# Down projections: loads of residual rows and of the third product's operands held behind the operand unit in use

## The chip, the core and the metric

The kernel runs on one core of a Trainium2 chip. A core has five engines that run their own instruction queues: TensorE (PE in the profile; its weight loads are PEld), VectorE (DVE), ScalarE (ACT), GpSimd (POOL) and SyncE (SP), which here issues nearly all transfers between DRAM and the on-chip memory. The engines wait for each other through semaphores; an instruction that waits holds up everything behind it in the same queue. The metric is the device time of one execution in microseconds; lower is better. It is given as the median of several runs, and one more execution is recorded by the hardware profiler.

## The reference

The program is a decoder trunk of two layers over 1024 tokens with 1024 features. The first layer mixes tokens with a gated linear recurrence, the second with sliding-window attention; both end with a gated feed-forward network, and every sub-layer is followed by a layer norm of a scaled residual. What matters here is the end of each layer:

```python
def conv_ffn(h, w_in, conv_w, conv_b, w_out):
    u = h @ w_in                                   # 1024 -> 2 * 2816
    u = <causal depthwise convolution of width 3>(u) + conv_b
    a, b = jnp.split(u, 2, axis=-1)
    return (jax.nn.silu(a) * b) @ w_out            # 2816 -> 1024

    # in reference(), for each layer:
    h = layer_norm(ALPHA * h + mix, ln_mix_g[layer], ln_mix_b[layer])
    ff = conv_ffn(h, ffn_w_in[layer], ffn_conv_w[layer], ffn_conv_b[layer], ffn_w_out[layer])
    h = layer_norm(ALPHA * h + ff, ln_ffn_g[layer], ln_ffn_b[layer])
```

All arrays are float32. The change is in how the last product, the down projection with `w_out`, is fed.

## The kernel before

**Split operands.** Each float32 operand is split into an upper half of reduced precision (`split`, L216, a cast on ScalarE) and the rest (`low_part`, L164, a subtract on VectorE). A product is then three matmuls (`mm3`, L189 to L191: upper by upper, upper by lower, lower by upper), into one bank of the accumulator memory.

**The up projection** (`Up`) computes 22 blocks of 128 features for both halves of the gate, applies the convolution (L483 on ScalarE, L485 on VectorE) in tiles `Y[:, 0..6]`, multiplies the halves (L490) and writes each block to DRAM as `gd` (L491). The tile `Y[:, 7]` serves as a buffer for weights. Before it, the normalised mixer output, which is the residual of this sub-layer, was written to DRAM as `ynd`, eight rows of tiles of 512 KB each, because Y was needed for the convolution.

**The down projection** (`Down`) multiplies the 1024 x 2816 gate output with `w_out` by a scheme of seven half-size products in place of eight, in the order `ORDER = [1, 2, 5, 6, 7, 3, 4]`; here they are called the first to the seventh. Each sums over 11 operand units (H = 11). A unit (`operands`, L554) is a 128 x 512 block of the gate output and one of the weights, 256 KB each, or sums of such blocks. It is loaded by SP into one of four raw buffers (three `rx` and one `rd`, in turn), cast to its upper half by ScalarE (L216) and its rest is made by VectorE (L164). The result goes to one of 15 operand slots, in `HL`, `HT` and `T`. The third product adds two blocks (L569) in a tile `R`, which holds a pair of 128 x 512 blocks for each of the 11 units: `R[:, 0, k]` is loaded from `gd` (L544), `R[:, 1, k]` from sums of weights that were made earlier and stand in DRAM as `bsd` (L552).

**The steps.** A step is one `mm3`: one unit k with one of four token blocks tb, that is four banks to a product and 44 steps to a product, about 0.68 us each. The steps go through the units in order, four steps each, for the first six units (`late` is 6 in the first product); then tb by tb through units 6 to 10. So units 6 to 10 are met in five steps in a row, 24 to 28. The banks of a product are emptied into Y (`evacuate`, L605 to L609), those of products 1 and 2 through a list `later`.

**The residual.** Before anything is added to it, Y must hold the residual rows: each is loaded from `ynd` (L652), multiplied by the gain row and shifted by the bias row of the layer norm before (L653, two instructions on VectorE a row, called shifts here). These two rows of parameters are loaded (L295) into parts of R: `free_rows(3)` and `free_rows(4)` are `R[:, 0, 6..7]` and `R[:, 0, 8..9]`. The shifts stand first in the list `later`; `run` takes one from the list after steps 11, 15, 19 and so on, in the order of rows 0, 4, 1, 5, 2, 6, 3, 7. A row's load is called together with its first shift.

**What sets the order.** Only TensorE's queue is in the order in which the code is written:

```python
    with tile.TileContext(nc) as tc, tc.manual_schedule(engines={mybir.EngineType.PE}):
```

In the down projections the queues of the other engines are laid out when the kernel is built: a planner runs through a modelled time and gives each engine, whenever it is free, an instruction whose operands are ready then, the one that was called earliest first. Loads with a free destination can so come long before the place where they are called. On the chip the laid-out order is fixed. `ahead` holds units 0 to 2 of the first product, which are called during the last block of the up projection.

Of the kernel before, what the change touches and what calls it, by code (L numbers as in the profile page):

```python
# [10 lines left out]
F32 = mybir.dt.float32  # L11
# [96 lines left out]
def trunk(ctx: ExitStack, tc: tile.TileContext, a: dict, out: bass.AP):  # L108
    nc = tc.nc
# [11 lines left out]
    Y = cp.tile([P, 8, D], F32, name="Y")  # L121
# [8 lines left out]
    ynd = drp.tile([P, 8, D], F32, name="ynd")  # L130
# [57 lines left out]
    def mm3(ps, st, mv, start, stop, n=512):  # L188
        nc.tensor.matmul(ps, st(0), mv(0), start=start, stop=False)  # L189
        nc.tensor.matmul(ps, st(0), mv(1), start=False, stop=False)  # L190
        nc.tensor.matmul(ps, st(1), mv(0), start=False, stop=stop)  # L191
        od.t += 3 * n / 2365.0
# [100 lines left out]
    def row_tiles(tiles, g, b):  # L293
        for r, v in zip(tiles, (g, b)):
            nc.sync.dma_start(r, bass.AP(tensor=v.tensor, offset=v.offset, ap=[[0, P], [1, D]]))  # L295
        return tiles
# [74 lines left out]
    class Up:  # L371
        def __init__(self, l, pool, rx):
            self.l, self.rx = l, rx
            self.wv = a["ffn_w_in"][l].rearrange("(kc p) c -> p kc c", p=P)
            self.TX = pool.tile([P, 3, 2, 4, 512], F32R, name="TX")
            self.W, self.raw, self.pieces = {}, {}, 0
# [67 lines left out]
        def product(self, p, fc, ps):  # L444
            TX = self.TX
            moving = {1: lambda j, k: T[:, j, k, :512], 2: lambda j, k: T[:, j, 4 + k, :512],
                      3: lambda j, k: TX[:, 1, j, k, :], 4: lambda j, k: T[:, j, 4 + k, 512:],
                      5: lambda j, k: T[:, j, k, 512:], 6: lambda j, k: TX[:, 0, j, k, :],
                      7: lambda j, k: TX[:, 2, j, k, :]}[p]
            block = {1: 0, 2: 1, 5: 2, 4: 3, 7: 4, 6: 5, 3: 6}[p]  # L450
            ws = self.W[fc]
            fixed = lambda j, k: (ws[6][:, 512 * j + 128 * k:512 * j + 128 * k + 128] if block == 6 else
                                  ws[block // 2 * 2 + j][:, 512 * (block % 2) + 128 * k:512 * (block % 2) + 128 * k + 128])
            for k in range(4):
                mm3(ps, lambda j: fixed(j, k), lambda j: moving(j, k), k == 0, k == 3)
                od.tick()
            return ps
# [35 lines left out]
        def run(self, ready, down):  # L493

            od.finish(ready[:4])
            tiles = [psax(), psax()]
            ax = [tiles[i % 2][:, i // 2 * 512:(i // 2 + 1) * 512] for i in range(4)]

            for (p, fc), ps in zip([(p, fc) for p in (4, 5) for fc in range(2)], ax):
                self.product(p, fc, ps)  # L500
            od.finish(ready[4:])
            mm = [psmm() for _ in range(4)]
            self.pairs = [mm, ax]
            for (p, fc), ps in zip([(p, fc) for p in (1, 2) for fc in range(2)], mm):
                self.collect(p, fc, self.product(p, fc, ps))
            for fc in range(2):
                self.collect(6, fc, self.product(6, fc, mm[fc]))
            for fc in range(2):
                self.collect(7, fc, self.product(7, fc, mm[2 + fc]))
                self.collect(4, fc, ax[fc])  # L510
                self.collect(5, fc, ax[2 + fc])
            self.weight_load(2)
            for fc in range(2):
                self.product(3, fc, mm[fc])
                if fc == 0:
                    self.weight_sums(2)
                self.collect(3, fc, mm[fc])
            banks, n = mm[2:] + ax[:2] + mm[:2] + ax[2:], 0
            for fc in range(2, NF):
                if fc > 2:  # L520
                    self.weights(fc)
                for p in (1, 2, 6, 7, 4, 5, 3):
                    self.collect(p, fc, self.product(p, fc, banks[n % 8]))
                    n += 1
                    if fc == NF - 1 and p in (1, 6, 4):
                        down.ahead.append(down.operands(0, len(down.ahead)))

    class Down:
# [3 lines left out]
        def __init__(self, l, raw):  # L532
            self.last = l == 1
            self.w, self.sums, self.tasks, self.ahead = a["ffn_w_out"][l], bsd[l], [], []
            self.raw = list(raw)

        def begin(self, pool, banks):
            self.banks = banks
# [79 lines left out]
        def product(self, i, ln):  # L618
            p, H = self.ORDER[i], self.H
            banks = self.banks[i % 2]  # L620
            hls, late = dict(enumerate(self.ahead)) if i == 0 else {}, H - (4 if p == 4 or self.last and p == 3 else 5)
            if self.last and p == 4:
                late = 0
            held = []
            steps = [(k, tb) for k in range(late) for tb in range(4)]
            for k, tb in steps + [(k, tb) for tb in range(4) for k in range(late, H)]:
                if k not in hls:
                    hls[k] = self.operands(i, k)
                hl = hls[k]
                mm3(banks[tb], lambda j: hl[:, j, 0, tb * P:(tb + 1) * P], lambda j: hl[:, j, 1, :],  # L630
                    k == 0, k == H - 1)
                od.tick()
                if k == H - 1:
                    if i < 2:
                        self.later.append(lambda p=p, tb=tb: self.evacuate(p, tb, banks[tb], ln))
                    elif self.last and p == 3:
                        held.append(tb)
                        if tb > 1:
                            self.evacuate(p, held.pop(0), banks[tb - 2], ln)
                    else:  # L640
                        self.evacuate(p, tb, banks[tb], ln)
                yield
            for tb in held:
                self.evacuate(p, tb, banks[tb], ln)

        def run(self, mid_rows, end_rows, ln):
            self.later = []
            rows = row_tiles([self.free_rows(3 + j) for j in range(2)], *mid_rows)

            def shift(tb, r, op):  # L650
                if r is rows[0]:
                    nc.sync.dma_start(Y[:, tb, :], ynd[:, tb, :])  # L652
                tt(Y[:, tb, :], Y[:, tb, :], r, op=op)  # L653

            for tb in (0, 4, 1, 5, 2, 6, 3, 7):
                for r, op in zip(rows, (ALU.mult, add)):
                    self.later.append(lambda tb=tb, r=r, op=op: shift(tb, r, op))
            for i in range(7):
                for n, _ in enumerate(self.product(i, ln)):
                    if n % 4 == 3 and 44 * i + n > 8 and self.later:  # L660
                        self.later.pop(0)()
                    if i == 5 and n == 20 and end_rows is not None:
                        row_tiles([self.free_rows(j) for j in range(2)], *end_rows)
            return self.tasks
# [835 lines left out]
```

## Time and profile before

| | us |
|---|---|
| median of 3 runs | 2197.13 |
| lowest and highest | 2196.31, 2198.64 |
| the profiled execution's own time | 2197.87 |
| its span in the trace | 2196.1 |
| the first layer's down projection begins | 1012.85 |
| the second layer's down projection begins | 1974.83 |
| mean granted clock of TensorE | 0.998 |

The span runs from the first to the last recorded instruction; the execution's own time is 1.8 us longer. The trace gives each instruction its start and its duration, and for idle time in front of an instruction what ended it: "0.62 <-ACT T L216" means that the engine stood idle for 0.62 us until ScalarE's instruction of line 216 on tile T was done. A group such as "x3" is three like instructions in a row. Matmuls are pipelined, so a recorded matmul of 0.39 us is followed by the next after 0.23 us; a gap is read from start to start. Names such as `rx`, `rd`, `HL`, `T`, `R` and `Y` are the program's tiles, `psmm` and `psax` the accumulator banks.

### The profile page before, as it was taken

To read this page: it belongs to the slowest core of one execution; us is meant where nothing else is said; L and a number is where in the kernel's file an instruction comes from. 1 tells how busy PE (TensorE), PEld (TensorE's weight loads), DVE (VectorE), ACT (ScalarE), POOL (GpSimd) and SP (SyncE) were. 2 spreads that over 40 slices of the span, in tenths; PEclk is the share of its full clock that TensorE was granted. 3 is DMA by queue.
4 is the path that set the end of the run, shared out by engine and by line. 5 is a ranking of instruction groups with operands and counts; after the bars stand their busy time and mean duration, and the time that the engine had idled before them with its cause. 6 is when DMAs were issued, how large, how long until landed. Compare 5 with 4: busy or idle time off the path is not lost.

```text
span 2196.1 us, 33273 instructions
## 1 busy us (share of the span) xinstructions
PE 2166.0 (99%) x13168; PEld 1810.5 (82%) x13168; DVE 1763.6 (80%) x2392; ACT 923.4 (42%) x1568; POOL 132.5 (6%) x161
## 2 busy tenths in 40 slices
PE   9999999989999999999999999999999999999998
PEld 8888888978788888887888888878888888887887
DVE  3776666566789888888998659978899988889987
ACT  3333333342844433444333256745644444343431
POOL 0000000030100000000001113211000000000001
PEclk9999999999999999999999999999999999999999
DMA  5654543243222222227855411123133222249663
GB/s 196 231 174 160 187 135 116 72 81 131 87 86 82 83 87 87 87 91 258 288 179 191 119 32 37 32 95 118 58 107 95 87 77 71 82 155 315 204 216 130
DMA packets 231685, 281.15 MB, mean 128 GB/s; under 512 B 29977, under 2 KB 160745, under 8 KB 228713
## 3 DMA queue, kind: packets, MB, share of 16 engines
q1 hardware_dynamic: 228448, 276.53, 38.8%
q10 hardware_dynamic: 2888, 2.45, 0.9%
q8 instruction: 103, 1.69, 0.3%
q14 instruction: 54, 0.43, 0.1%
q0 software_dynamic: 192, 0.04, 0.0%
HBM read 213.96 MB, written 65.01 MB: 127 GB/s over the span
## 4 chain that ended last, share of the span: by engine, by line
PE 78%; DVE 11%; DMA 4%; ACT 3%; issue 2%; POOL 1%; SPq 0%; ACTq 0%; DVEq 0%; POOLq 0%
PE psmm L189 16%; PE psmm L191 15%; PE psmm L190 15%; PE psax L189 8%; PE psax L191 8%; PE psax L190 8%; PE psax L195 3%; DVE HL L164 1%; DVE T L164 1%; PE psax L199 1%; PE psmm L195 1%; DVE Y L485 1%; DMA rx<-in_ffn_w_in_dram 1%; PE psax L1295 1%; DMA raw<-in_hgrn_w_out_dram 1%
## 5 line engine op out<-in xcount | busy, mean ns | idle before, releaser
L189 PE MATMUL psmm<-T,HL 128*128 128x512 f32 x768 | 307.2, 400 | 0.0
L190 PE MATMUL psmm<-T,HL 128*128 128x512 f32 x768 | 300.0, 391 | 2.1 <-DVE T L164 2.1
L191 PE MATMUL psmm<-T,HL 128*128 128x512 f32 x768 | 300.6, 391 | 0.0
L485 DVE SCALAR_TENSOR_TENSOR Y<-Y,cwt 128x1023 f32<-128x1023 f32 (+1 forms) x176 | 225.0, 1278 | 40.3 <-ACT Y L483 40.1
L483 ACT ACTIVATE Y<-Y,cwt 128x1024 f32<-128x1024 f32 x88 | 108.9, 1238 | 263.8 <-DVE Y L472 260.6
L189 PE MATMUL psmm<-HL,T 128*128 128x256 f32 (+1 forms) x656 | 199.0, 303 | 0.0
L191 PE MATMUL psmm<-HL,T 128*128 128x256 f32 (+1 forms) x656 | 195.0, 297 | 1.1 <-DVE T L164 1.1
L190 PE MATMUL psmm<-HL,T 128*128 128x256 f32 (+1 forms) x656 | 194.9, 297 | 0.0
L216 ACT CAST HL<-rx 128x1024 fp32r<-128x1024 f32 (+1 forms) x137 | 140.3, 1044 | 124.0 <-DMA rx<-in_ffn_w_in_dram 35.1
L164 DVE TENSOR_TENSOR HL<-rx,HL 128x1024 fp32r<-128x1024 f32 (+1 forms) x137 | 165.5, 1211 | 14.3 <-ACT HL L216 13.8
L190 PEld LDWEIGHTS psmm<-T,HL 128*128 128x128 f32 x768 | 144.4, 188 | 31.1 <-DVE T L164 2.9
L191 PEld LDWEIGHTS psmm<-T,HL 128*128 128x128 f32 x768 | 144.2, 188 | 31.1
L189 PEld LDWEIGHTS psmm<-T,HL 128*128 128x128 f32 x768 | 144.3, 188 | 30.1 <-issue 0.4
L191 PE MATMUL psax<-T,HL 128*128 128x512 f32 x352 | 137.6, 391 | 0.0
L189 PE MATMUL psax<-T,HL 128*128 128x512 f32 x352 | 137.5, 391 | 0.0
L190 PE MATMUL psax<-T,HL 128*128 128x512 f32 x352 | 137.4, 390 | 0.0
L164 DVE TENSOR_TENSOR HL<-raw,HL 128x1024 fp32r<-128x1024 f32 x52 | 63.8, 1228 | 90.1 <-ACT HL L171 89.9
L189 PEld LDWEIGHTS psmm<-HL,T 128*128 128x128 f32 x656 | 126.2, 192 | 6.1 <-issue 2.5
L191 PEld LDWEIGHTS psmm<-HL,T 128*128 128x128 f32 x656 | 126.1, 192 | 4.7 <-DVE T L164 1.5
L190 PEld LDWEIGHTS psmm<-HL,T 128*128 128x128 f32 x656 | 126.2, 192 | 3.2
L238 POOL TENSOR_TENSOR rs<-rs,nhalf 128x1 f32<-128x1 f32 x32 | 33.2, 1039 | 1309.5 <-DVE rs L237 1309.1
L216 ACT CAST HT<-rx 128x1024 fp32r<-128x1024 f32 (+1 forms) x51 | 43.8, 859 | 89.5 <-PE psmm L190 30.6
(296 smaller groups left out, 5188.1 us busy)
## 6 DMA issues: line engine op xcount, KB each, us to landing
rx<-in_ffn_w_in_dram SPq DMA_DIRECT2D x136, 256.0 KB, 3.4
rx<-gd SPq DMA_DIRECT2D x118, 256.0 KB, 3.8
Y<-in_ffn_w_out_dram SPq DMA_DIRECT2D x44, 512.0 KB, 6.0
bsd<-Y SPq DMA_DIRECT2D x22, 1024.0 KB, 4.2
gd<-Y SPq DMA_DIRECT2D x44, 512.0 KB, 2.7
rx<-in_ffn_w_out_dram SPq DMA_DIRECT2D x54, 256.0 KB, 4.2
R<-bsd SPq DMA_DIRECT2D x44, 256.0 KB, 4.1
Y<-in_ffn_w_in_dram SPq DMA_DIRECT2D x40, 256.0 KB, 3.4
```

Of the source, the lines that this page charges most:

```text
L164: make = lambda e: e.tensor_tensor(lo, src, hi.bitcast(F32), op=ALU.subtract)
L189: nc.tensor.matmul(ps, st(0), mv(0), start=start, stop=False)
L190: nc.tensor.matmul(ps, st(0), mv(1), start=False, stop=False)
L191: nc.tensor.matmul(ps, st(1), mv(0), start=False, stop=stop)
L195: nc.tensor.matmul(ps, lhsT, rhs, start=start, stop=stop, **kw)
L199: nc.tensor.transpose(ps, src, ident)
L216: nc.scalar.copy(hi, src)
L238: nc.gpsimd.tensor_tensor(rs, rs, nhalf, op=ALU.pow)
L483: nc.scalar.activation(c, u, AF.Identity, bias=cwt[:, l, 3, ci:ci + 1], scale=cwt[:, l, 2, ci:ci + 1])
L485: nc.vector.scalar_tensor_tensor(c[:, sh:], u[:, :S - sh], cwt[:, l, 2 - sh, ci:ci + 1], c[:, sh:], op0=ALU.mult, op1=ALU.add)
L1295: nc.tensor.matmul(pv[:, e, jj, lo:], q[bp // 2][es, e, qs], Kl[es, pp, ks] if low else Kh[:, pp, e, ks], start=not low and jj == 0, stop= ...
```

## The change

A row's load is no longer called with its first shift. It is a function of its own, `residual`, called after steps 4, 11, 18, 25, 32, 39, 46 and 53. Ahead of the load, GpSimd copies one element (of each partition) of the upper half of the operand unit in use into the first column of the row's tile. The load overwrites that column, so it has to wait for the copy, and the copy waits for the cast of the unit. The unit in use is kept in `self.unit`; it is the last unit called, and unit 0 until unit 3 is called (step 12), since units 0 to 2 come from `ahead`.

In the same way, when a unit k of the second product is called, GpSimd copies one element into each of the two blocks of R that the third product's unit k will be loaded to; for k from 6 to 9 only into the second, since the first holds the rows of the layer norm.

The shifts are taken from the list after steps 18, 21, 25, 28, 32, 35 and so on (two in seven), in place of one in four from step 11 on. There are 8 copies for rows and 11 for R in each of the two down projections. Nothing that is computed changes.

```diff
--- before.py
+++ after.py
@@ -532,7 +532,7 @@
         def __init__(self, l, raw):
             self.last = l == 1
             self.w, self.sums, self.tasks, self.ahead = a["ffn_w_out"][l], bsd[l], [], []
-            self.raw = list(raw)
+            self.raw, self.unit = list(raw), None

         def begin(self, pool, banks):
             self.banks = banks
@@ -626,6 +626,10 @@
             for k, tb in steps + [(k, tb) for tb in range(4) for k in range(late, H)]:
                 if k not in hls:
                     hls[k] = self.operands(i, k)
+                    self.unit = hls[k]
+                    if i == 1:
+                        n = slice(1 if k in (6, 7, 8, 9) else 0, 2)
+                        nc.gpsimd.tensor_copy(self.R[:, n, k, 0:1], hls[k][:, 0, n, 0:1].bitcast(F32))
                 hl = hls[k]
                 mm3(banks[tb], lambda j: hl[:, j, 0, tb * P:(tb + 1) * P], lambda j: hl[:, j, 1, :],
                     k == 0, k == H - 1)
@@ -646,18 +650,26 @@
         def run(self, mid_rows, end_rows, ln):
             self.later = []
             rows = row_tiles([self.free_rows(3 + j) for j in range(2)], *mid_rows)
+            self.unit = self.ahead[0]

             def shift(tb, r, op):
-                if r is rows[0]:
-                    nc.sync.dma_start(Y[:, tb, :], ynd[:, tb, :])
                 tt(Y[:, tb, :], Y[:, tb, :], r, op=op)

-            for tb in (0, 4, 1, 5, 2, 6, 3, 7):
+            def residual(tb):
+
+                nc.gpsimd.tensor_copy(Y[:, tb, 0:1], self.unit[:, 0, 0, 0:1].bitcast(F32))
+                nc.sync.dma_start(Y[:, tb, :], ynd[:, tb, :])
+
+            order = (0, 4, 1, 5, 2, 6, 3, 7)
+            for tb in order:
                 for r, op in zip(rows, (ALU.mult, add)):
                     self.later.append(lambda tb=tb, r=r, op=op: shift(tb, r, op))
             for i in range(7):
                 for n, _ in enumerate(self.product(i, ln)):
-                    if n % 4 == 3 and 44 * i + n > 8 and self.later:
+                    step = 44 * i + n
+                    if step < 60 and step % 7 == 4:
+                        residual(order[step // 7])
+                    if step >= 18 and step % 7 in (0, 4) and self.later:
                         self.later.pop(0)()
                     if i == 5 and n == 20 and end_rows is not None:
                         row_tiles([self.free_rows(j) for j in range(2)], *end_rows)
```

## The prediction

> **What bounds the kernel now.** I read the page first, then the list of what TensorE waited for, then TensorE's, VectorE's and the DMA queue's own order of time around the two down projections, and at the end the busy time of each engine over a stretch that I cut from those. The page, first the span, then the busy time of the engines:
>
> ```profile
> span 2196.1 us, 33273 instructions
> PE 2166.0 (99%) x13168; PEld 1810.5 (82%) x13168; DVE 1763.6 (80%) x2392; ACT 923.4 (42%) x1568; POOL 132.5 (6%) x161
> ```
>
> TensorE is busy for 2166.0 of 2196.1 us. The change adds and removes no matmul, so it can win only TensorE's idle time, 30 us in the whole kernel, and of this only what lies where it acts. These are the places in the two down projections where one matmul does not follow the last at the usual 0.23 us. Columns: start, duration, engine, line, operation, and in brackets the idle time and what ended it.
>
> ```profile
> 1012.85 0.39 PE L189 MATMUL psmm<-HL 128*128 128x512 f32 x1
> ...
> 1031.78 0.39 PE L191 MATMUL psmm<-T 128*128 128x512 f32 x1
> 1032.79 0.50 PE L189 MATMUL psmm<-T 128*128 128x512 f32 x1 [0.62 <-ACT T L216]
> 1034.05 0.50 PE L190 MATMUL psmm<-T 128*128 128x512 f32 x1 [0.76 <-DVE T L164]
> ...
> 1127.99 0.39 PE L191 MATMUL psax<-T 128*128 128x512 f32 x1
> 1128.37 0.50 PE L189 MATMUL psax<-T 128*128 128x512 f32 x1
> ...
> 1974.83 0.39 PE L189 MATMUL psmm<-HL 128*128 128x512 f32 x1
> ...
> 1993.76 0.39 PE L191 MATMUL psmm<-T 128*128 128x512 f32 x1
> 1994.46 0.50 PE L189 MATMUL psmm<-T 128*128 128x512 f32 x1 [0.31 <-ACT T L216]
> 1995.72 0.50 PE L190 MATMUL psmm<-T 128*128 128x512 f32 x1 [0.76 <-DVE T L164]
> ...
> 2089.71 0.39 PE L191 MATMUL psax<-T 128*128 128x512 f32 x1
> 2091.09 0.50 PE L189 MATMUL psax<-T 128*128 128x512 f32 x1 [0.99 <-DVE Y L609]
> ```
>
> From 1012.85 to 1031.78 are 83 matmuls of 0.228 us. So the matmul at 1032.79 is the 85th, the first of step 28, where the first product meets its last operand unit (number 10). It waits for the unit's upper half, the next one for its lower half: 1.01 + 1.26 - 2 x 0.23 = 1.81 us lost. In the second layer it is 0.70 + 1.26 - 0.46 = 1.50 us. The second place is step 34 of the fourth product: 0.38 - 0.23 = 0.15 us in the first layer, 1.38 - 0.23 = 1.15 us in the second, where L609 empties a bank. Together 4.61 us, 0.21% of the time: more than this can't be won here. A measurement of this kernel tells about 0.2% (4.4 us) from no change.
>
> What decides is which of the two places ends last. I cut each down projection from its first matmul to the second place. Columns: length, then busy time and instructions of PE, PEld, DVE, ACT, POOL, the granted clock, the busy share of the DMA engines, GB/s.
>
> ```profile
> 1012.85:1128.37 115.52, 114.14 (x500) 93.22 (x498) 112.06 (x121) 46.59 (x46) 0.00 (x0) 1.00 0.77 259
> 1974.83:2091.09 116.26, 114.20 (x500) 93.23 (x498) 112.12 (x121) 46.58 (x46) 0.00 (x0) 1.00 0.77 257
> ```
>
> VectorE works 112.06 and 112.12 us in them, with 121 instructions both times: it idles 3.46 us in the first and 4.14 us in the second. The stretches differ by 0.74 us, VectorE's idle times by 0.68. So VectorE, not TensorE, sets when the second place is reached: the wait at unit 10 is made good by a shorter one at step 34. Taking away the wait at step 28 alone moves nothing at the end; a gain is what VectorE idles less, up to 1.96 us (the waits 1.81 + 0.15) in the first layer and 2.65 us in the second. These are VectorE's idle times that matter, and the order around them:
>
> ```profile
> 1017.17 1.23 DVE L653 TENSOR_TENSOR Y<-Y,R 128x1024 f32<-128x1024 f32 x1 [0.27 <-DMA R<-in_ln_mix_g_dram]
> ...
> 1021.84 1.22 DVE L653 TENSOR_TENSOR Y<-Y,R 128x1024 f32<-128x1024 f32 x1
> ...
> 1024.11 1.22 DVE L653 TENSOR_TENSOR Y<-Y,R 128x1024 f32<-128x1024 f32 x1
> 1025.24 1.22 DVE L164 TENSOR_TENSOR HL<-rd,HL 128x1024 fp32r<-128x1024 f32 x1
> ...
> 1032.77 1.22 DVE L164 TENSOR_TENSOR T<-rd,T 128x1024 fp32r<-128x1024 f32 x1 [0.63 <-ACT T L216]
> ...
> 1053.86 1.23 DVE L164 TENSOR_TENSOR HL<-rx,HL 128x1024 fp32r<-128x1024 f32 x1 [0.42 <-ACT HL L216]
> ...
> 1125.89 0.69 DVE L579 TENSOR_TENSOR rx<-rx,R 128x512 f32<-128x512 f32 x1 [1.00 <-DMA rx<-gd]
> ...
> 1127.63 0.68 DVE L609 TENSOR_TENSOR Y<-Y,psax 128x512 f32<-128x512 f32 x1
> ...
> 1994.44 1.23 DVE L164 TENSOR_TENSOR T<-rd,T 128x1024 fp32r<-128x1024 f32 x1 [0.47 <-ACT T L216]
> 1996.11 3.50 DVE L653 TENSOR_TENSOR Y<-Y,R 128x1024 f32<-128x1024 f32 x3 [0.44 <-DMA Y<-ynd]
> ...
> 2013.72 1.22 DVE L164 TENSOR_TENSOR HL<-rx,HL 128x1024 fp32r<-128x1024 f32 x1 [0.49 <-ACT HL L216]
> ...
> 2019.23 1.23 DVE L164 TENSOR_TENSOR HL<-rx,HL 128x1024 fp32r<-128x1024 f32 x1 [0.89 <-ACT HL L216]
> ```
>
> **The change part by part.** First the order of the shifts (L653). They are called after steps 11, 15, 19, 23 and so on, and after the change at 18, 21, 25, 28. In the rows above, the last shift called before step 24 (the fourth, 1024.11) still stands ahead of the subtract of unit 6 (1025.24), which step 24 calls. With the new calls only two shifts are older than unit 6. (The emptying of the first product's banks, called from step 75 on, is called from 74 on: no price.) Its subtract frees the buffer that unit 10 is loaded into, so I let it move up by one or two instructions of 1.14 us (the distance from 1024.11 to 1025.24). Second, the loads:
>
> ```profile
> 1013.04 0.33 SPq L295 DMA_DIRECT2D R<-in_ln_mix_g_dram  x1
> ...
> 1016.77 0.51 SPq L652 DMA_DIRECT2D Y<-ynd  x1
> ...
> 1024.59 0.43 SPq L652 DMA_DIRECT2D Y<-ynd  x1
> ```
>
> ```profile
> 1026.85 4.76 DMA rd<-in_ffn_w_out_dram
> ```
>
> ```profile
> 1010.30 1.03 ACT L216 CAST HL<-rx 128x1024 fp32r<-128x1024 f32 x1
> ...
> 1054.91 1.05 ACT L216 CAST HL<-rx 128x1024 fp32r<-128x1024 f32 x1 [1.08 <-DMA rx<-in_ffn_w_out_dram]
> ```
>
> A row load is 512 KB; at the 259 GB/s of the stretch that is 2.0 us of all DMA engines. The second half of unit 10's load took 4.76 us to land, with row 6 ahead of it. The gates are less tight than they look: the first two stand on unit 0, which was cast long before, the third (row 1) on unit 4, cast at 1010.30, the fourth (row 5) on unit 7, the next two (rows 2 and 6) on unit 10, the last two (rows 3 and 7) on the first and third unit of the second product. By the order in which the up projection lets go of Y's tiles, the loads at 1016.77 and 1024.59 are rows 2 and 6; they leave the time before unit 10. Unit 10 needs its upper half 0.78 us and its lower half 1.81 us earlier. With its load called 1.14 to 2.3 us earlier and up to 2 us less traffic ahead of it, I take this wait as gone: VectorE's 0.63 and 0.47 us go, and the 0.44 us of the late row load in the second layer, 1.54 us in all. The late units of the second product (0.42, 0.49 and 0.89, together 1.80) wait for loads that share the DMA engines with the third product's; these are spread by the new gates but not reduced, so nothing and all of it are the bounds, and I take half, 0.90.
>
> What it costs: row 1 no longer goes early, but at about 1011 to 1013, into the queue ahead of the rows of the layer norm (1013.04), on which the first shift already waits 0.27 us. The bounds are nothing and one whole load, 2.0 us, in each layer. I take 0.5, nearer to the row that stands there, because the convolution's instructions, which now come after the first shift, can go before it. Two layers: 1.0 us.
>
> The gates on R. They come with the second product's units; the last of those is cast at 1054.91, and its load follows some 1 + 0.6 us later and takes 4.76. VectorE first touches R at 1065.19:
>
> ```profile
> 1065.19 0.68 DVE L569 TENSOR_TENSOR R<-R,rd 128x512 f32<-128x512 f32 x1
> ```
>
> Even that last load lands at 1061.3, before the third product's first add, though it is only wanted ten units later. So I cost it at nothing; the cover is 3.9 us, and if the second product's units came that much later, each further microsecond would stop VectorE. In the queue of SP a held load stands before later unit loads, and a gate that opens late holds those too; I cost this at nothing, since a unit is cast before its buffer is free for the next load, and the third rival is what it costs if the order is another.
>
> The copies: 8 for rows and 11 for R in each layer, 38 in all, on POOL, which does nothing in the stretches (0.00 above). The nearest rows, of small POOL instructions, the columns being the shortest, median and longest in ns:
>
> ```profile
> L238 POOL TENSOR_TENSOR rs<-rs,nhalf x32: 550/1340/1462, 543.5 to 2190.3; 128x1 f32<-128x1 f32 x32
> ```
>
> ```profile
> L1317 POOL TENSOR_TENSOR se<-sk,nm x24: 202/203/205, 1290.7 to 1416.0; 128x4 f32<-128x4 f32 x24
> ```
>
> ```profile
> 1191.83 1.28 DVE L275 SCALAR_TENSOR_TENSOR Y<-Y,mv,R 128x1024 f32<-128x1024 f32 x1
> 1193.02 0.68 DVE L609 TENSOR_TENSOR Y<-Y,psax 128x512 f32<-128x512 f32 x1
> ```
>
> ```profile
> 464.25 2.87 DVE L898 TENSOR_TENSOR kp<-kp,tot 128x512 f32<-128x512 f32 x1
> ```
>
> So a gate opens 0.2 to 1.5 us after its unit's cast; nobody waits for the row so soon. For VectorE the bounds are nothing (an L238 ran beside the instruction at 1191.83, and the next came 1.19 us later, as everywhere) and 0.20 us a copy. I take nothing: those are the like size, 128x1. But a large POOL instruction stretched a VectorE one to 2.87 us at 464.25. The Trainium skill ("SBUF — State Buffer", Who interferes with whom) says that VectorE instructions with two SBUF inputs and GpSimd instructions that read SBUF lock each other out for a whole instruction. The trace agrees for the large ones and shows no such loss for the small; by that rule the copies would cost VectorE their length each, the second rival below.
>
> Sum: -1.54 - 0.90 + 1.0 = -1.44 us. The profiled execution took 2197.87 us, which gives 2196.43; the median of the runs, 2197.13, is 0.74 lower, so 2195.7 us. What is late next: the bank that L609 empties at step 34, as before.
>
> **Rivals.** (1) The loads gain everything: VectorE idles at least 1.96 and 2.65 us less. For it speaks that the idle times above sum to 1.3 in the first layer (0.27, 0.63, 0.42) and 2.3 in the second, against it that this is less than wanted. 2197.1 - 4.6 = 2192.5. (2) The port: each copy stops VectorE for 0.20 us; 38 x 0.20 = 7.6, so 2195.7 + 7.6 = 2203.3, slower. (3) VectorE stands for a held row. A row's load now comes some 14 steps before its shift is called, but the shifts run when VectorE's planned order puts them, and a planned order that counts on a row landing sooner makes VectorE stop, for nothing else may pass. The 0.44 us at 1996.11 are such a stop. Four rows a layer (5, 2, 6, 7) come late; two stops a layer of half of the 4.76 us, 2.4 each, make 9.6, less the 2.4 gained: 2197.1 + 9.6 - 2.4 = 2204, slower. From 2.2 us of new idle time a layer beyond the gains it makes the change slower. (4) It does little: half of the gates are open at once, SP has the unit loads to issue before those of R, as now, and what unit 10 gains, the layer norm's rows lose: 2197.
>
> **How the numbers follow.** Chances: the forecast 0.45, (4) 0.18, (1) 0.10, (2) 0.07, (3) 0.20. Faster by over 0.2% is under 2192.7: half of (1) and a little of the forecast, 0.06. Slower by over 0.2% is above 2201.5: (2) and most of (3), 0.25. The rest, 0.69, is within 0.2%. The range begins at 2192.5, where all waits are gone, and goes up to 2202, so that only the upper parts of (2) and (3) lie outside. The likeliest case alone spans 2193.8 (all 1.80 of the late units gained, and no loss at the layer norm's rows: 2195.7 - 0.9 - 1.0) to 2199.6 (none gained, and both rows' loads lost in full: + 0.9 + 3.0).
>
> **What the changed profile would show.** TensorE's wait at step 28 under 0.5 us in both layers; the subtract of unit 6 ahead of the third shift; two row loads fewer between 1016 and 1026; stretches of 114.8 and 115.5 us with VectorE still busy 112.1. Wrong: a shift that waits for Y's load by 1 us or more, VectorE instructions that last longer beside POOL, SP's queue standing at a held load while a unit's buffer is free, or TensorE waiting in the second or third product, where it waits for nothing now.

## The result, and the profile after

The changed kernel takes 2209.28 us (median of 6 runs, 2207.61 to 2214.51) against 2197.53 us of the kernel before (6 runs, 2196.19 to 2198.64): a ratio of 1.0052, with a 95% interval of 1.0041 to 1.0063. It is slower by half a per cent, where the forecast was no change to be measured. The profiled execution took 2209.67 us. The page of the changed kernel, first the span, then the engines' busy time:

```profile
span 2207.9 us, 33362 instructions
PE 2169.7 (98%) x13168; PEld 1812.9 (82%) x13168; DVE 1764.1 (80%) x2392; ACT 922.7 (42%) x1568; POOL 168.4 (8%) x199
```

The span grew by 11.8 us; VectorE's work stayed the same (1763.6 before). The order of time of TensorE in the changed kernel shows where the time lies (columns as in the prediction):

```profile
1033.51 0.39 PE L191 MATMUL psmm<-T 128*128 128x512 f32 x1
1040.75 0.80 PE L189 MATMUL psmm<-T 128*128 128x512 f32 x1 [6.85 <-ACT T L216]
1042.01 0.80 PE L190 MATMUL psmm<-T 128*128 128x512 f32 x1 [0.46 <-DVE T L164]
...
1043.02 0.63 PE L189 MATMUL psmm<-HL 128*128 128x512 f32 x1
...
1047.29 0.50 PE L190 MATMUL psmm<-T 128*128 128x512 f32 x1
...
1138.75 0.39 PE L189 MATMUL psax<-T 128*128 128x512 f32 x1
...
2004.67 0.39 PE L189 MATMUL psmm<-T 128*128 128x512 f32 x1
2005.57 0.50 PE L190 MATMUL psmm<-T 128*128 128x512 f32 x1 [0.52 <-DVE T L164]
...
2066.88 0.50 PE L190 MATMUL psmm<-HT 128*128 128x512 f32 x1 [0.77 <-DVE HT L164]
...
2102.03 0.50 PE L189 MATMUL psax<-T 128*128 128x512 f32 x1 [0.91 <-DVE Y L609]
```

Most of it lies at the place that the change was expected to mend: step 28 of the first product, where TensorE meets unit 10. In the first layer it now waits 7.24 + 1.26 - 2 x 0.23 = 8.0 us, where it waited 1.81. In the second layer the wait did shrink, to 0.90 - 0.23 = 0.67 us from 1.50, but TensorE now also waits 1.1 us in the third product (before 2066.88), where it waited for nothing before. Behind the long wait comes a second loss: from 1042.01 to 1047.29 the matmuls follow each other at 0.44 us on average (twelve in 5.28 us) instead of 0.23, another 2.5 us. The windows of the changed kernel show why, and give the two stretches that the prediction cut (columns as there; the seventh after the length is the granted clock):

```profile
1014.58:1138.75 124.17, 116.86 (x499) 95.42 (x498) 112.02 (x120) 45.44 (x45) 20.26 (x16) 0.96 0.73 248
1985.51:2102.03 116.52, 114.33 (x500) 93.15 (x498) 111.46 (x120) 45.31 (x45) 14.73 (x16) 1.00 0.79 262
1041.00:1045.00 4.00, 3.54 (x8) 2.47 (x9) 3.22 (x3) 0.00 (x0) 2.13 (x2) 0.50 0.51 152
1049.00:1053.00 4.00, 4.00 (x19) 3.31 (x18) 2.61 (x4) 2.25 (x3) 1.34 (x2) 1.00 0.91 339
```

After the 7 us of idleness the granted clock stands at 0.50 and is back at 1.00 by 1049. The Trainium skill ("TensorE: Matmul & The Clock Gate", Part 1) says that the clock is halved after an idle window of about 3.4 us and returns after as long a time of work; the trace agrees in kind, but here the matmuls stay slow until 6.5 us after the first one. In the kernel before, none of the waits in these stretches lowered it (1.00 in both).

The first stretch took 115.52 us and now takes 124.17 (+8.65); the second 116.26 and 116.52 (+0.26). The rest of the span's 11.8 us: +1.73 ahead of the first down projection, +0.30 between the two stretches, +0.86 after the second. I can't put the first of these down to the change: over the profiled executions of the versions below the first down projection begins anywhere from 1011.97 to 1015.41, and one that begins at 1014.94 takes 2197.1 us in all, as long as the kernel before.

What holds unit 10 back is read from the queues of the changed kernel in order of time: GpSimd, VectorE, SP's DMA queue, ScalarE.

```profile
1023.41 9.01 POOL L660 COPY Y<-T 128x1 f32<-128x1 f32 x1 [6.28 <-DVE Y L485]
...
1023.21 1.22 DVE L656 TENSOR_TENSOR Y<-Y,R 128x1024 f32<-128x1024 f32 x1
1024.34 1.22 DVE L490 TENSOR_TENSOR Y<-Y 128x1024 f32<-128x1024 f32 x1
1025.48 1.22 DVE L164 TENSOR_TENSOR HL<-rd,HL 128x1024 fp32r<-128x1024 f32 x1
...
1031.15 1.22 DVE L164 TENSOR_TENSOR T<-rx,T 128x1024 fp32r<-128x1024 f32 x1
1040.73 1.23 DVE L164 TENSOR_TENSOR T<-rd,T 128x1024 fp32r<-128x1024 f32 x1 [8.35 <-ACT T L216]
...
1019.79 0.54 SPq L544 DMA_DIRECT2D rx<-gd  x1
1032.44 0.33 SPq L661 DMA_DIRECT2D Y<-ynd  x1
...
1033.76 1.40 SPq L548 DMA_DIRECT2D rd<-in_ffn_w_out_dram  x1
1035.58 7.90 SPq L661 DMA_DIRECT2D Y<-ynd  x4
...
1039.65 1.04 ACT L216 CAST T<-rd 128x1024 fp32r<-128x1024 f32 x1 [11.76 <-DMA rd<-in_ffn_w_out_dram]
```

The copy for row 3's gate, one element in each partition, begins at 1023.41 and takes 9.01 us. VectorE runs eight instructions with two inputs in that time without a break, from 1023.21 to 1032.37, and the copy ends when VectorE has nothing ready any more. In SP's planned order row 3's load stands ahead of unit 10's. So SP issues nothing from 1019.79 to 1032.44, although unit 10's buffer has been free since 1026.70, the end of the subtract of unit 6 (1025.48). Unit 10's weights go out at 1033.76, are cast at 1039.65, and TensorE goes on at 1040.75. The list of SP's waits in this part has the same in one line (us in total, times, the longest):

```profile
SPq L661 <- POOL Y L660: 15.8, 5, 11.0
```

The same copy in the second layer began beside the same VectorE instruction and got in at its end, after 1.06 us. VectorE's stops that follow it there are of another kind, for unit 10's cast and for held rows:

```profile
1994.53 1.06 POOL L660 COPY Y<-T 128x1 f32<-128x1 f32 x1 [6.13 <-issue]
...
2004.29 1.23 DVE L164 TENSOR_TENSOR T<-rd,T 128x1024 fp32r<-128x1024 f32 x1 [0.79 <-ACT T L216]
2007.41 1.23 DVE L656 TENSOR_TENSOR Y<-Y,R 128x1024 f32<-128x1024 f32 x1 [0.76 <-DMA Y<-ynd]
2009.84 4.63 DVE L656 TENSOR_TENSOR Y<-Y,R 128x1024 f32<-128x1024 f32 x4 [1.20 <-DMA Y<-ynd]
```

### The profile page after: what moved, and what is told of

It reads as the page before. It is cut to its first block, busy times and chain, and to the rows that moved or that the text cites. A ratio compares the mean times of both kernels' runs of the same rounds, so it can differ in the third digit from the quotient of the medians.

```text
span 2207.9 us, 33362 instructions
## 1 busy us (share of the span) xinstructions
PE 2169.7 (98%) x13168; PEld 1812.9 (82%) x13168; DVE 1764.1 (80%) x2392; ACT 922.7 (42%) x1568; POOL 168.4 (8%) x199
## 4 chain that ended last, share of the span: by engine, by line
PE 78%; DVE 11%; DMA 4%; ACT 3%; issue 3%; POOL 1%; SPq 0%; ACTq 0%; DVEq 0%; POOLq 0%
PE psmm L189 16%; PE psmm L191 15%; PE psmm L190 15%; PE psax L191 8%; PE psax L189 8%; PE psax L190 8%; PE psax L195 3%; DVE T L164 1%; DVE HL L164 1%; PE psax L199 1%; PE psmm L195 1%; DVE Y L485 1%; PE psax L1307 1%; DMA raw<-in_hgrn_w_out_dram 1%; ACT Y L264 1%
## 5 line engine op out<-in xcount | busy, mean ns | idle before, releaser
L189 PEld LDWEIGHTS psax<-T,HL 128*128 128x128 f32 x352 | 66.1, 188 | 14.2
```

## The experiments

Theory 1, formed on this trace: row 3's copy is shut out for as long as VectorE runs two-input instructions back to back, SP stands at the row's load behind it, and unit 10 is late (theory A in the later expectations). Rivals: the holding of the loads costs time by itself, however quickly the copies run; the copies slow VectorE; the new places of the calls cost time; the copies on R do it. The kernel before ran beside each group on the same chip (medians 2198.32, 2198.05 and 2197.65 us); ratios are to it.

**Row 3's gate reads nothing.** For row 3 alone the copy becomes a memset; every other instruction of all queues keeps its place.

```diff
-                nc.gpsimd.tensor_copy(Y[:, tb, 0:1], self.unit[:, 0, 0, 0:1].bitcast(F32))
+                if tb == 3:
+                    nc.gpsimd.memset(Y[:, tb, 0:1], 0.0)
+                else:
+                    nc.gpsimd.tensor_copy(Y[:, tb, 0:1], self.unit[:, 0, 0, 0:1].bitcast(F32))
```

> The changed kernel, but row 3's gate is a GpSimd memset of the same element, which reads nothing (so it doesn't wait for its unit, whose cast is long past). SP's, VectorE's and ScalarE's queues are in the same order as in the changed kernel. Theory 1 (a GpSimd copy that reads on-chip memory doesn't get in while VectorE runs two-input instructions back to back; the copy of row 3 took 9.0 us, and SP stood at row 3's load with unit 10's load behind it): the memset takes 0.2 us, TensorE's 7 us wait at step 28 of the first layer and the slow clock behind it go, about 8 us less: 2200 to 2202. Theory 2 (the order of SP's queue alone, with held loads ahead of unit 10's, makes unit 10 late): no change, 2208 to 2210.

Measured: 2201.87 us, ratio 1.0021 (1.0011 to 1.0031). In the order of time of this kernel, GpSimd and VectorE in the first layer:

```profile
1022.05 0.10 POOL L661 MEMSET Y<- 128x1 f32 x1 [6.36 <-DVE Y L485]
1025.77 7.58 POOL L632 COPY R<-T 128x2 f32<-128x2 f32 x1 [3.62 <-ACT T L216]
...
1021.86 1.23 DVE L656 TENSOR_TENSOR Y<-Y,R 128x1024 f32<-128x1024 f32 x1
1038.55 3.65 DVE L656 TENSOR_TENSOR Y<-Y,R 128x1024 f32<-128x1024 f32 x3 [5.25 <-DMA Y<-ynd]
```

The memset takes 0.10 us in the middle of a two-input instruction of VectorE (1021.86 to 1023.09); the wait at step 28 is gone, and with it 7 us. But the loss isn't gone: now the next copy on R is shut out for 7.58 us, row loads behind it in GpSimd's and SP's queues come late, and VectorE stands 5.25 us for one.

**Row 3's gate reads something else.** To see whether it is the reading that counts or the unit that is read, row 3's copy reads a constant that was written at the start.

```diff
-                nc.gpsimd.tensor_copy(Y[:, tb, 0:1], self.unit[:, 0, 0, 0:1].bitcast(F32))
+                gate = nhalf if tb == 3 else self.unit[:, 0, 0, 0:1].bitcast(F32)
+                nc.gpsimd.tensor_copy(Y[:, tb, 0:1], gate)
```

> The changed kernel, but row 3's gate copies from a constant that was written at the start, in place of the operand unit; all queues in the same order. Theory 1: it still reads, so it is still shut out while VectorE runs without a pause, a copy of several us, 2208 to 2210. If the copy had waited for its unit: a copy of 0.2 us and 2200 to 2202.

Measured: 2211.42 us (4 runs, 2207.97 to 2216.84), ratio 1.0063 (1.0041 to 1.0085). GpSimd and TensorE in both layers; the trace is of the slowest of the four executions:

```profile
1021.79 9.01 POOL L661 COPY Y<-nhalf 128x1 f32<-128x1 f32 x1 [6.02 <-DVE Y L485]
1994.17 9.01 POOL L661 COPY Y<-nhalf 128x1 f32<-128x1 f32 x1 [6.33 <-issue]
...
1039.39 0.79 PE L189 MATMUL psmm<-T 128*128 128x512 f32 x1 [7.11 <-ACT T L216]
2011.76 0.80 PE L189 MATMUL psmm<-T 128*128 128x512 f32 x1 [7.11 <-ACT T L216]
```

The same 9.01 us, here in both layers, with the same wait at step 28. It isn't the unit that is late, but the copy's read. The Trainium skill ("SBUF — State Buffer", Who interferes with whom) says that a VectorE instruction with two SBUF inputs contends with a GpSimd instruction that reads SBUF and not with one that only writes. These two runs agree: 9.01 us for the copy, 0.10 us for the memset.

**No copies at all.** The calls stay in their new places, the two lines with the copies are out.

```diff
-                    if i == 1:
-                        n = slice(1 if k in (6, 7, 8, 9) else 0, 2)
-                        nc.gpsimd.tensor_copy(self.R[:, n, k, 0:1], hls[k][:, 0, n, 0:1].bitcast(F32))
...
-                nc.gpsimd.tensor_copy(Y[:, tb, 0:1], self.unit[:, 0, 0, 0:1].bitcast(F32))
```

> The changed kernel without any of the 38 copies: loads of rows called on their own and shifts called later stay, nothing is held. Theory 1: no long wait at step 28 in the first layer (under 2 us), the time is that of the kernel before within 2 us: 2195.5 to 2199.5. Theory 3 (the new places of the calls are what costs): 2204 or more.

Measured: 2197.58 us, ratio 0.9996 (0.9987 to 1.0006). TensorE no longer waits at step 28 in either layer, but at step 34 of the fourth product of this kernel it does:

```profile
1130.38 0.50 PE L189 MATMUL psax<-T 128*128 128x512 f32 x1 [0.97 <-DVE Y L609]
...
2092.86 0.50 PE L189 MATMUL psax<-T 128*128 128x512 f32 x1 [1.10 <-DVE Y L609]
```

So the whole loss comes with the copies. The new places of the calls take TensorE's wait at step 28 away and gain nothing that can be measured: in the first layer the wait at step 34 grows from 0.15 to 1.13 us. VectorE's own stops haven't gone. It still stands 0.83 us for unit 10's cast in the first layer (0.63 before), and now for a row, though no load is held:

```profile
1036.75 3.50 DVE L653 TENSOR_TENSOR Y<-Y,R 128x1024 f32<-128x1024 f32 x3 [1.11 <-DMA Y<-ynd]
```

**Copies that nobody waits for.** All 38 copies are made, into a tile of their own, with the loads not held.

```diff
...
-                nc.gpsimd.tensor_copy(Y[:, tb, 0:1], self.unit[:, 0, 0, 0:1].bitcast(F32))
+                nc.gpsimd.tensor_copy(self.spare[:, 0, tb, 1:2], self.unit[:, 0, 0, 0:1].bitcast(F32))
```

> As without copies, but with all 38 copies going to a spare tile that nothing reads; SP's, VectorE's and ScalarE's queues are in the same order as without copies. Theory 1: some copies take several us, VectorE's instructions keep their length, and the time is that without copies within 1 us. The rival of the prediction that each copy stops VectorE: VectorE's busy time in the down projections grows by up to 0.2 us a copy, 3 to 8 us more in the time.

Measured: 2197.79 us, ratio 0.9999 (0.9989 to 1.0008). The two largest groups of these copies on GpSimd (shortest, median and longest in ns):

```profile
L633 POOL COPY spare<-HL x12: 257/1022/1249, 1041.1 to 2022.5; 128x2 f32<-128x2 f32 x6, 128x1 f32<-128x1 f32 x6
L661 POOL COPY spare<-T x10: 178/1196/1242, 1015.0 to 2003.9; 128x1 f32<-128x1 f32 x10
```

VectorE's work doesn't grow: 111.29 and 111.34 us from the first matmul to the second place, against 111.08 and 111.33 without copies, where the rival had 3 to 8 us more. The copies took at most 1.26 us each here, where theory 1 had expected several us for some: without a tile to wait for, none fell into VectorE's unbroken row ahead of unit 10. So this run doesn't test whether it matters where a copy writes, and it doesn't show what a long one does to VectorE (the 1.22 us of its instructions beside the 9.01 us above does: they last no longer than elsewhere).

**Only the copies on R, and only those for the rows.** The first leaves out the row copies, the second the copies on R.

```diff
-                nc.gpsimd.tensor_copy(Y[:, tb, 0:1], self.unit[:, 0, 0, 0:1].bitcast(F32))
```

> The 22 copies into R alone, no copies for rows; SP's, VectorE's and ScalarE's queues are in the same order as without copies. Theory 1: the third product's loads stand behind the unit loads in SP's queue anyway, and no copy is shut out for long when its unit is cast late in a pause of VectorE: 2196.5 to 2199, as without copies (2197.6). If the gates on R cost: 2200 or more.

Measured: 2197.43 us, ratio 0.9999 (0.9990 to 1.0009). The 22 copies on R cost nothing without the others.

```diff
-                    if i == 1:
-                        n = slice(1 if k in (6, 7, 8, 9) else 0, 2)
-                        nc.gpsimd.tensor_copy(self.R[:, n, k, 0:1], hls[k][:, 0, n, 0:1].bitcast(F32))
```

> Only the 16 copies of the row gates are left, the 22 copies on R are out; SyncE, VectorE and ScalarE keep the order of the changed kernel. Theory A (row 3's copy is shut out while VectorE runs two-input instructions back to back, and SyncE's queue stands at row 3's load): the whole loss stays, 2206 to 2211 us, with row 3's copy taking 7 to 10 us in the first layer and SyncE's wait for it over 10 us. Rival (the loss needs the copies on R too, as they fill GpSimd's queue ahead of row 3's): 2197 to 2202 us.

Measured: 2215.27 us (4 runs, 2209.94 to 2216.86), ratio 1.0076 (1.0063 to 1.0090). The whole loss, and more, is in the 16 row gates. GpSimd and TensorE in the first layer; the trace is of the fastest of the four executions (2209.94):

```profile
1021.66 8.92 POOL L657 COPY Y<-T 128x1 f32<-128x1 f32 x1 [10.18 <-DVE Y L485]
...
1039.23 0.79 PE L189 MATMUL psmm<-T 128*128 128x512 f32 x1 [7.17 <-ACT T L216]
```

In the second layer of this execution row 3's copy took 4.37 us. Its slower executions, and the spread of the run with the constant, would fit a copy that is shut out in one layer or in both, as it happens; with one trace of each kernel this isn't shown.

**The gates that were shut out, opened.** Row 3's gate and that of R's unit 2 become memsets, row 7's is copied by ScalarE; SP and VectorE keep their order.

```diff
-                        nc.gpsimd.tensor_copy(self.R[:, n, k, 0:1], hls[k][:, 0, n, 0:1].bitcast(F32))
+                        (nc.gpsimd.memset(self.R[:, n, k, 0:1], 0.0) if k in (2,) else nc.gpsimd.tensor_copy(self.R[:, n, k, 0:1], hls[k][:, 0, n, 0:1].bitcast(F32)))
...
-                nc.gpsimd.tensor_copy(Y[:, tb, 0:1], self.unit[:, 0, 0, 0:1].bitcast(F32))
+                if tb == 3: nc.gpsimd.memset(Y[:, tb, 0:1], 0.0)
+                elif tb == 7: nc.scalar.copy(Y[:, tb, 0:1], self.unit[:, 0, 0, 0:1].bitcast(F32))
+                else: nc.gpsimd.tensor_copy(Y[:, tb, 0:1], self.unit[:, 0, 0, 0:1].bitcast(F32))
```

> The changed kernel with row 3's gate a memset, row 7's gate copied by ScalarE, and the gate on R's unit 2 a memset; the other 33 copies stay on GpSimd, and the queues of SP and VectorE are in the same order as in the changed kernel. Theory 1 (copies that are shut out, and SP standing behind them, are the whole cost): with the copies that were shut out for 4 to 9 us replaced, what was left over in the first such run (2201.9) goes too: 2196 to 2199.5. If holding the loads costs by itself: 2201 to 2203, as with row 3 alone.

Measured: 2201.74 us, ratio 1.0013 (1.0004 to 1.0023), where theory 1 alone had expected the kernel before's time. No copy is shut out for more than 2.3 us, and still some 0.13% is lost. VectorE and SP's DMA queue of this kernel:

```profile
1035.54 1.23 DVE L656 TENSOR_TENSOR Y<-Y,R 128x1024 f32<-128x1024 f32 x1 [0.63 <-DMA Y<-ynd]
1038.02 4.63 DVE L656 TENSOR_TENSOR Y<-Y,R 128x1024 f32<-128x1024 f32 x4 [1.25 <-DMA Y<-ynd]
...
1028.23 7.06 SPq L663 DMA_DIRECT2D Y<-ynd  x4
1035.39 0.38 SPq L544 DMA_DIRECT2D rx<-gd  x1
```

VectorE stops twice for a held row, and SP issues no unit load between 1028.23 and 1035.39, while it works off the four held rows. So the loss has two parts: about 7 us (2209.28 against 2201.87) hang on row 3's one copy, and about 3 us (0.13% of 2198) remain with the other gates. That these 3 us are due to the held rows is argued from VectorE's stops for rows (1.88 us here, 1.96 in the second layer, against 1.11 and 0.57 without copies), and not shown by a run of its own.

**The copies on ScalarE.** All of them; the planner lays the queues out anew.

```diff
...
-                nc.gpsimd.tensor_copy(Y[:, tb, 0:1], self.unit[:, 0, 0, 0:1].bitcast(F32))
+                nc.scalar.copy(Y[:, tb, 0:1], self.unit[:, 0, 0, 0:1].bitcast(F32))
```

> All 38 copies by ScalarE in place of GpSimd; the planner lays the queues out anew. Theory 1: ScalarE is not shut out by VectorE, so there is no copy of more than 0.5 us and no wait of 7 us at step 28: 2196 to 2201, with some cost for casts that stand behind a copy whose tile is not free. If the hold or the order is what costs: 2205 or more.

Measured: 2197.91 us, ratio 1.0002 (0.9992 to 1.0011). ScalarE's copies for the rows in the first layer of this kernel, and TensorE at step 28:

```profile
L660 ACT COPY Y<-T x5: 185/187/192, 1023.5 to 1032.8; 128x1 f32<-128x1 f32 x5
```

```profile
1032.73 0.49 PE L189 MATMUL psmm<-T 128*128 128x512 f32 x1 [0.72 <-ACT T L216]
1033.99 0.50 PE L190 MATMUL psmm<-T 128*128 128x512 f32 x1 [0.77 <-DVE T L164]
```

None takes over 0.2 us, and the time is that of the kernel before. The loads are held as in the change, so holding needn't cost anything; but the wait at step 28 is back as well (0.88 + 1.03 us), so it brings nothing either. VectorE stands for held rows here too (1.21 us in the first layer, 1.49 in the second) without a loss of time, which speaks against the held rows as the whole of the 3 us. As the order of the loads differs here, this doesn't say how much of the 3 us above is due to the order.

**A pause in VectorE's queue.** Behind each shift VectorE is to set one element of a tile of its own, an instruction that reads nothing. The planner is free to move these memsets, and it puts the first two ahead of all shifts.

```diff
...
-                tt(Y[:, tb, :], Y[:, tb, :], r, op=op)
+                tt(Y[:, tb, :], Y[:, tb, :], r, op=op); nc.vector.memset(self.pause, 0.0)
```

> The changed kernel with a one-element memset of VectorE, on a tile of its own, behind each of its 32 shifts: an instruction that reads nothing. The order of the planned queues shifts a little with it. Theory A1 (GpSimd's copy gets in whenever VectorE runs something other than a two-input instruction): no copy takes over 2.5 us, since one shift lies within every two or three instructions there; time 2199 to 2203 us, what the held rows cost by themselves. Rival A2 (GpSimd's copy gets in only when VectorE's queue stands idle, whatever VectorE runs): copies of 4 to 9 us remain, 2203 to 2211 us.

Measured: 2201.26 us, ratio 1.0017 (1.0008 to 1.0026). GpSimd, VectorE and TensorE of this kernel:

```profile
1022.80 3.33 POOL L660 COPY Y<-T 128x1 f32<-128x1 f32 x1 [7.74 <-DMA rx<-gd]
...
1024.88 1.21 DVE L656 TENSOR_TENSOR Y<-Y,R 128x1024 f32<-128x1024 f32 x1
...
1026.04 0.06 DVE L656 MEMSET pause<- 128x1 f32 x1
...
1034.71 0.50 PE L189 MATMUL psmm<-T 128*128 128x512 f32 x1 [2.80 <-ACT T L216]
```

Row 3's copy, the longest of all, ends at 1026.13, just after a memset (1026.04) that stands behind the first shift (1024.88 to 1026.09) that VectorE began beside it. My bound of 2.5 us was too low, for the instruction that was running and another one lie ahead of that shift, but the copy no longer waits until VectorE's queue stands still. The planned queues differ a little from the changed kernel's, so this supports the reading without settling it. Nor is the time that of the held rows alone: in the first layer TensorE still loses 3.18 + 1.26 - 2 x 0.23 = 3.98 us at step 28, and behind it the granted clock is 0.50 (1036 to 1039).

**The second place.** Two kernels empty the fourth product's banks two token blocks later, where step 34 no longer waits for them: one without copies and with the new places of the calls (run twice, in two groups), one that is otherwise the kernel before.

```diff
-                    elif self.last and p == 3:
+                    elif self.last and p == 3 or i == 3:
```

> Without copies, and the fourth product's banks are emptied two token blocks later in the order of the calls, so that the matmuls of step 34 no longer stand behind the emptying of a bank that shares their tile. Theory (VectorE sets the second place through that wait): the waits at step 34 and 39 (1.1 + 0.4 and 1.3 + 0.5 us) go, 1 to 3 us less than without copies: 2194.5 to 2196.5. If VectorE is late for everything there, the wait moves to the next operands: 2197 to 2198.

> The version without copies, with the new places of the calls and the late emptying, once more with more rounds: both waits gone, 2195 to 2196.5 us, a ratio of 0.9990 to 0.9995 to the kernel before. If the earlier result was chance: ratio 1.000.

> The kernel before with one edit that has nothing to do with the loads: the banks of the fourth product are emptied two token blocks later, as in the version without copies. If the wait at step 34 and the wait at step 28 are two separate losses (0.15 + 1.15 us and 1.81 + 1.50 us), the first goes and the second stays: 2196 to 2197.5 us. If VectorE sets the second place as the prediction has it, the wait at step 28 is then no longer made good and the gain is at most 1.3 us.

Measured: without copies 2196.36 us, ratio 0.9992 (0.9983 to 1.0002), and the second time 2195.30 us, ratio 0.9989 (0.9980 to 0.9998); the kernel before with late emptying 2196.23 us, ratio 0.9993 (0.9984 to 1.0002). In the trace of the first no wait of TensorE over 0.7 us is left in the two down projections; in the last, step 34 is free and step 28 waits as ever:

```profile
1031.76 0.50 PE L189 MATMUL psmm<-T 128*128 128x512 f32 x1 [0.47 <-ACT T L216]
1033.02 0.50 PE L190 MATMUL psmm<-T 128*128 128x512 f32 x1 [0.76 <-DVE T L164]
```

The version without copies is the fastest that was run, by 1.7 and 2.4 us, which only the second run can tell from no change. Whether the new places of the calls add anything to the late emptying isn't settled by the times: the intervals overlap almost entirely. In the traces the two stretches sum to 227.4 and 227.8 us with both edits, 230.2 with the late emptying alone and 230.0 with the new places alone, against 231.8 before. That looks like two separate gains; but the version with copies that nobody waits for, whose time is that without copies, has 232.5, so one trace of each can't settle it either.

## Why the prediction was wrong, point by point

- **What bounds the kernel** held in part. VectorE's busy time in the stretches stayed near 112 us (112.02 and 111.46). Without the copies the wait at step 28 goes, step 34 waits about a microsecond, and the time doesn't change measurably. With the emptying moved as well the time falls by 1.7 and 2.4 us, within the 4.6 us that the prediction gave as the most; with the emptying alone moved it falls by 1.4, which the interval doesn't tell from these. So the prediction's "moves nothing at the end", for the wait at step 28 alone, agrees with the times but can't be told from a gain of 1 or 2 us.
- **Fewer shifts ahead of unit 6** was right. The subtract of unit 6 began 12.39 us after the first matmul (1025.24 - 1012.85) and now begins 10.90 us after it (1025.48 - 1014.58), 1.5 us earlier, inside the 1.14 to 2.3. In the second layer the wait at step 28 shrank to 0.67 us. In the first it was of no use, for SP didn't issue the load.
- **The gains** (-1.54 and -0.90) didn't come. In the second layer of the changed kernel, where no copy beside these stops took over 1.25 us, VectorE stood 0.79 us for unit 10 (0.47 before), 0.76 + 1.20 for rows (0.44) and 1.65 for late units of the second product (1.38): 4.4 us in place of 2.3. Without the copies the same places of both layers sum to 5.5 us, 3.3 before. Earlier calls of the loads did not make VectorE idle less there; why the planned order gave this isn't shown.
- **The step that failed is the one on SP's queue**: "I cost this at nothing, since a unit is cast before its buffer is free". The premise was about the unit, and the unit was in time; the gate is not open when the unit is cast but when the copy is done, and the copy took 9.01 us. The price was 6.2 us of waiting at step 28 (8.0 instead of 1.81) and 2.5 us of the slower clock. The prediction named the sign of it ("SP's queue standing at a held load while a unit's buffer is free") but left its price to the third rival, which is about VectorE standing for a row and has no term for unit 10.
- **Under it lies the bound of the copy's length**, 0.2 to 1.5 us from the small instructions of L1317 and L238. Those rows were of the right size but stood in another company: the bound left out how long VectorE can go on without a break. The rows for that were in the profile before: VectorE's queue around 1024 holds little but two-input instructions of 1.22 us. The prediction used the rule of the shared lock only in one direction, for VectorE losing time. The trace shows the other: VectorE's instructions stayed at 1.22 us, and GpSimd waited. So the second rival (0.20 us a copy for VectorE) falls.
- **VectorE standing for a held row**, the third rival, happened at a smaller size: stops of 0.76 and 1.20 us in the second layer of the changed kernel and of 0.63 and 1.25 us in the first with the gates open, in place of two of 2.4 us a layer. At most the 3 us that remain with the gates open are its price, in place of 7.
- **Row 1's load ahead of the layer norm's rows** (+1.0) didn't happen: the stop of 0.27 us at the first shift is absent from the changed kernel, and the version without copies, where it is 0.27 us as before, loses nothing.
- **The gates on R at nothing** was right for themselves (0.9999), though one of these copies, shut out, holds the rows behind it in the version with the memset.

What stays open: why a copy gets in at one seam of VectorE's instructions and not at the next. In the second layer row 3's copy got in after 1.06 us between the same two instructions where it didn't in the first, and with the other source it was shut out in both. Others got in after one, two or three ends of VectorE's instructions (2.26, 3.33 and 4.37 us).

## What to carry to other kernels

A wait that is made of a tiny instruction lasts until that instruction gets its turn, not as long as its work: ask what its engine can be shut out by, and put such a gate on an engine that isn't (0.2 us a copy on ScalarE here), or make it an instruction that reads nothing (0.10 us here). When a load is held, read the queue behind it: here one element held back unit 10 for 7 us, and the idle time cost a third as much again in TensorE's clock. And where two waits lie on one engine's path, look at the second when you take away the first: here step 34's wait in the first layer grew from 0.15 to 1.13 us when step 28's 1.81 went.

## What was unexpected of the hardware

GpSimd copies of one or two elements a partition, 0.2 us when alone, stood 9.01, 9.01, 9.01, 8.92 and 7.58 us beside VectorE's two-input instructions, past six or seven of their ends, and finished only when VectorE had nothing to run; most of the other copies finished at the first such end, in 1.3 us at most. The Trainium skill ("SBUF — State Buffer", SBUF: two separate sides) says that the one that comes second is blocked for the whole instruction of the other; these runs show that it can be blocked for a whole row of them. And 7 us without a matmul brought the granted clock to 0.50, with matmuls at nearly half their rate until 6.5 us after the restart; in the version with the pause a gap of 3.18 us and one of 1.26 behind it were enough for 0.50.
